# Two 64x64 products in two quarters of TensorE: a second set of operands in the other half of the partitions

## The chip, the cores and the metric

The kernel runs on one core of a Trainium2 chip. The metric is the device time of one execution in microseconds (us). The kernel before was timed three times, and once more under the profiler. The profile's engine names are PE (TensorE's matmuls), PEld (its weight loads), DVE (VectorE), ACT (ScalarE), POOL (GpSimd) and SP (SyncE, which here issues nearly all DMAs).

## The reference, cut to what matters

The reference is one inference step of a decoder layer with two branches, a gated delta rule and a sparse attention, for a prompt of 256 tokens and 8 x 8 sampled tokens. One input projection feeds both branches, and two output projections and a last one follow. Nearly all of TensorE's work is in these projections.

The change touches the delta rule alone, and in it the triangular system of each chunk and head:

```python
a_strict = jnp.where(strict, jnp.einsum('bhnid,bhnjd->bhnij', kb, k) * decay, 0.0)
rhs = jnp.concatenate([v * beta[..., None], kb * jnp.exp(G)[..., None]], axis=-1)
sol = lax.linalg.triangular_solve(a_strict, rhs, left_side=True, lower=True, unit_diagonal=True)
```

There are 32 value heads. Everything is in float32.

## The kernel before, in words

**The stream.** TensorE's main work is a stream of weight blocks of 128 columns, each in two halves (`stream`, line 379). SyncE loads a half into one of the `raw` buffers (`load_ahead`, 351), ScalarE and VectorE split it into a high and a low part, `whi` and `wlo` (`split_ahead`, 364), and 24 matmuls of 128x128 by 320 tokens add it up in a PSUM bank `pm`. A block's `done` function then reads the bank.

**Side work.** Everything else is written as Python generators. Twice per half (`side_round`, 297) each generator may emit its next step. The kernel keeps a clock of its own (`Clock`, 74) that books every instruction at an estimated cost, a DMA issue on SyncE at 0.55 us among them (172). A step that has yielded a time is taken up again when this clock's TensorE has reached it. A step that needs PSUM banks takes them from a ring of six, `ps` (`need`, 283, and `psum`, 277), and waits while the number that it asks for is not idle by the clock. `force` (321) is for the stream: where a `done` function needs a buffer that side work still holds, it runs the side steps at once, until the buffer is free. All engines work strictly in the order in which the program emits, so whatever a forced step waits for, the stream waits for too.

**The delta rule's groups.** The heads are handled in eight groups of two key heads (four value heads). In a group the stream brings two blocks of k, two of q, four of z and four of v. The prompt is cut in two chunks of 128, so a group has eight 128x128 triangular matrices of the prompt, and four more of the sampled tokens whose blocks are 16x16 and fit in the diagonal blocks of 32. `kq_gen` (1743) makes these twelve matrices in the tile `BT`, and then spawns `inverse` (1835), which leaves the transposed inverses in `XT`.

**The inverse.** It works by blocks:

- The four 32x32 diagonal blocks of the twelve matrices (48 of them) go through DRAM (`d_b`) into 48 partitions of the tile `blk`, and GpSimd inverts them by forward substitution in the tile `Xt` (`X` in the profile): 31 pairs of multiply and subtract. The inverses go out to DRAM twice, as `d_x[0]` and, transposed, as `d_x[1]`.
- Then SyncE loads what TensorE needs: `BO`, the 64x64 block off the diagonal, and `BD`, the two 32x32 blocks off the diagonal (both from `d_o`), `XT`'s diagonal blocks from `d_x[1]`, and `XB` from `d_x[0]`, the inverse of the upper 64x64 block, not transposed. `BO`, `BD`, `Q1` are slices of the tile `blk`, and `XB`, `Q2` of `Xt`. One fill by GpSimd clears a 32x32 corner of `XB`.
- Step 1 multiplies `BD` with `XB`'s diagonal blocks: 16 products of 32x32, in two quarters of the array in turn (rows 0 to 31 with columns 32 to 63, rows 64 to 95 with columns 96 to 127). Both write one bank, and ScalarE copies the result to `Q1`.
- Step 2 finishes the two 64x64 inverses: three products of 32x32 per matrix, 24 in all. Two give blocks of `XT`, the third the lower left block of `XB`. ScalarE copies them with the sign turned.
- Step 3 multiplies `BO` with `XB`: eight products of 64x64, all with rows 0 to 63 and columns 64 to 127. ScalarE copies the result to `Q2`, partitions 64 to 127.
- Step 4 multiplies `Q2` with `XT`'s lower diagonal block: eight products of 64x64, all with rows 64 to 127 and columns 0 to 63. ScalarE copies them with the sign turned to `XT`.

Which rows of the array a product takes is set by the partitions of its two operands, which columns by the PSUM partitions of its result.

**What follows.** `prompt_chain` (1968) and `sample_chain` (2045) of the group's two key heads start once `XT` is there. At their end they give back `vt` and, for the fourth use, `XT`. `v_gen` (1937) needs a free `vt` (there are two) and gives back the `vf` buffers (there are three) into which the convolution has written v. `v_done` (1693) takes a `vf` buffer for every v block and forces one where none is free. The tiles `blk` and `Xt` exist once, and so do `BT` and `XT`.

Of the kernel before, what the change touches and what calls it, by code (L numbers as in the profile page):

```python
# [11 lines left out]
AF = mybir.ActivationFunctionType  # L12
# [189 lines left out]
class Kernel:  # L202
# [1632 lines left out]
    def inverse(self, g, G):  # L1835
        nc = self.nc
        BT = G["BT"]
        d_b, d_x, d_o = self.d_b[g % 2], self.d_x[g % 2], self.d_o[g % 2]
        yield self.ready(BT)
        for k in range(4):  # L1840
            nc.sync.dma_start(d_b[k].rearrange("m j i -> j m i"), BT[32 * k:32 * k + 32, :, 32 * k:32 * k + 32])
        nc.sync.dma_start(d_o[:, :, 0:64], BT[0:64, 0:8, 64:128])
        for o in (0, 64):
            nc.sync.dma_start(d_o[o // 2:o // 2 + 32, :, 64:96], BT[o:o + 32, 0:8, o + 32:o + 64])
        self.BT.put(BT)
        yield
        yield from self.need(self.inv)
        tiles = blk, Xt = self.inv.get()
        yield self.idle(blk, Xt)
        nc.sync.dma_start(blk[0:48], d_b.rearrange("k m j i -> (k m) (j i)"))  # L1850
        nc.gpsimd.memset(Xt[0:48], 0.0)
        nc.gpsimd.memset(Xt[0:48, 0:1024:33], 1.0)
        yield
        X = Xt[0:48].rearrange("p (i c) -> p i c", c=32)
        B = blk[0:48].rearrange("p (j i) -> p j i", i=32)
        for j in range(31):
            n, m = 31 - j, j + 1
            t = self.tmp[:, 0:n * m].rearrange("p (i c) -> p i c", c=m)
            bv = B[:, j, j + 1:32].rearrange("p (i o) -> p i o", o=1).to_broadcast([48, n, m])
            xv = X[:, j:j + 1, 0:m].to_broadcast([48, n, m])  # L1860
            self.tt(t, bv, xv, OP.mult, eng=nc.gpsimd)
            self.tt(X[:, j + 1:32, 0:m], X[:, j + 1:32, 0:m], t, OP.subtract, eng=nc.gpsimd)
            if j % 4 == 4 - 1:
                yield self.clock.last - 3.6
        nc.gpsimd.tensor_copy(blk[0:48].rearrange("p (c i) -> p c i", i=32), X.rearrange("p i c -> p c i"))
        yield
        while not self.XT.free:
            yield
        XT = G["XT"] = self.XT.get()
        XB = Xt[:, 0:512].rearrange("p (m c) -> p m c", c=64)  # L1870
        Q2 = Xt[:, 512:1024].rearrange("p (m c) -> p m c", c=64)
        BO = blk[:, 0:512].rearrange("p (m c) -> p m c", c=64)
        BD = blk[:, 512:768].rearrange("p (m c) -> p m c", c=32)
        Q1 = blk[:, 768:1024].rearrange("p (m c) -> p m c", c=32)
        nc.sync.dma_start(d_x[0].rearrange("k m i c -> (k m) (i c)"), Xt[0:48])
        nc.sync.dma_start(d_x[1].rearrange("k m i c -> (k m) (i c)"), blk[0:48])
        yield max(self.clock.last, self.idle(XT))
        nc.gpsimd.memset(XB[0:32, :, 32:64], 0.0)
        nc.sync.dma_start(BO[0:64], d_o[:, :, 0:64])
        for o in (0, 64):  # L1880
            nc.sync.dma_start(BD[o:o + 32], d_o[o // 2:o // 2 + 32, :, 64:96])
        for k in range(4):
            s = slice(32 * k, 32 * k + 32)
            nc.sync.dma_start(XT[s, :, s], d_x[1][k].rearrange("m i c -> i m c"))
            if k < 3:
                o = 32 * (k % 2)
                nc.sync.dma_start(XB[s, :, o:o + 32], d_x[0][k, 0:8].rearrange("m i c -> i m c"))
        yield
        yield from self.need(self.ps_side)
        p = self.psum()  # L1890
        pv = p[:, 0:256].rearrange("p (m c) -> p m c", m=8)
        for m in range(8):
            for o in (0, 64):
                self.mm(pv[o + 32:o + 64, m, :], BD[o:o + 32, m, :], XB[o:o + 32, m, 0:32], skip=True)
        for o in (32, 96):
            self.act(Q1[o:o + 32], pv[o:o + 32])
        self.ps_side.put(p)
        yield
        yield from self.need(self.ps_side)
        p = self.psum()  # L1900
        pv = p.rearrange("p (e m c) -> p e m c", e=2, m=8)
        for m in range(8):
            for o in (0, 64):
                self.mm(pv[o:o + 32, 0, m, :], Q1[o + 32:o + 64, m, :], XT[o + 32:o + 64, m, o + 32:o + 64], skip=True)
            self.mm(pv[32:64, 1, m, :], XT[32:64, m, 32:64], Q1[32:64, m, :], skip=True)
        for o in (0, 64):
            self.act(XT[o:o + 32, 0:8, o + 32:o + 64], pv[o:o + 32, 0], AF.Copy, scale=-1.0)
        self.act(XB[32:64, :, 0:32], pv[32:64, 1], AF.Copy, scale=-1.0)
        self.ps_side.put(p)
        yield  # L1910
        yield from self.need(self.ps_side)
        p = self.psum()
        pv = p.rearrange("p (m c) -> p m c", m=8)
        for m in range(8):
            self.mm(pv[64:128, m, :], BO[0:64, m, :], XB[0:64, m, 0:64], skip=True)
        self.act(Q2[64:128], pv[64:128])
        self.ps_side.put(p)
        yield
        yield from self.need(self.ps_side)
        p = self.psum()  # L1920
        pv = p.rearrange("p (m c) -> p m c", m=8)
        for m in range(8):
            self.mm(pv[0:64, m, :], Q2[64:128, m, :], XT[64:128, m, 64:128], skip=True)
        self.act(XT[0:64, 0:8, 64:128], pv[0:64], AF.Copy, scale=-1.0)
        self.ps_side.put(p)
        self.inv.put(tiles)
        G["T"] = 4
        self.inverses += 1
# [454 lines left out]
```

## Time and profile before

| | us |
|---|---|
| median of three runs | 2191.76 |
| the three runs | 2191.92, 2191.76, 2189.55 |
| profiled execution | 2190.04 |
| its span, from the first instruction to the last | 2188.3 |
| PE busy in the span | 2157.9 |
| granted TensorE clock | 0.998 |

All instructions stand under line 61 in this profile, because one helper issues them; so they are told apart by engine, operation, and tiles: `ps<-X,blk 64*64 64x64` is a matmul that writes a `ps` bank from the tiles `X` and `blk`, over 64 rows and 64 columns of the array, with 64 columns streamed. Of the inverse, step 1 is `ps<-X,blk 32*32`, step 2 `ps<-XT,blk` and `ps<-blk,XT`, step 3 `ps<-X,blk 64*64`, and step 4 `ps<-XT,X`. A row of a timeline gives the start, the extent up to the last end, engine, operation and count; in brackets stands the idle time before it and what ended it. The ends of matmuls are modelled by the profile: they overlap, so an extent is longer than the time that an instruction keeps the next one off.

### The profile page before, as it was taken

The numbers are of one execution on the slowest core, as the hardware profiler recorded it, in microseconds if no ns is written. First come the engines' busy times: TensorE is split into PE (matmuls) and PEld (weight loads), VectorE is DVE, ScalarE is ACT, GpSimd is POOL, SyncE is SP. The second block draws the span as 40 slices with busy tenths as digits, with TensorE's granted clock in tenths as the row PEclk, the third lists the DMA queues.
The fourth block names the chain that finished last, engine by engine and source line by source line (L and its number), as shares of the span: only waits on it lengthen the run. The fifth ranks groups of instructions, "written<-read, shape, count | busy, mean of one in ns | idle before, by whom it ended". The sixth has DMA issues, their size and how long they took to land.

```text
span 2188.3 us, 43683 instructions
## 1 busy us (share of the span) xinstructions
PE 2157.9 (99%) x17151; PEld 2041.2 (93%) x17151; DVE 1384.4 (63%) x2807; ACT 1002.9 (46%) x2207; POOL 458.2 (21%) x624
## 2 busy tenths in 40 slices
PE   7999999999999999999999999999999999999997
PEld 6889988999888999899999999999999999999997
DVE  4665447789644477777777777777756545545543
ACT  3225464343343455474646464646445434233343
POOL 1000100000000008361717171717270000000000
PEclk9999999999999999999999999999999999999999
DMA  9985549765666667686768686867786966655562
GB/s 333 354 281 151 155 120 264 218 188 142 186 209 203 192 170 196 169 217 186 217 177 219 178 220 177 219 178 212 184 233 187 279 194 201 177 151 155 154 183 87
DMA packets 709839, 433.14 MB, mean 198 GB/s; under 512 B 67936, under 2 KB 697024, under 8 KB 707328
## 3 DMA queue, kind: packets, MB, share of 16 engines
q1 hardware_dynamic: 705536, 407.67, 66.1%
q0 software_dynamic: 3616, 21.02, 2.8%
q8 instruction: 135, 2.21, 0.4%
q10 hardware_dynamic: 480, 1.65, 0.2%
q14 instruction: 72, 0.59, 0.1%
HBM read 382.09 MB, written 47.89 MB: 196 GB/s over the span
## 4 chain that ended last, share of the span: by engine, by line
PE 67%; issue 23%; DVE 5%; DMA 3%; ACT 1%; SPq 0%; DVEq 0%; POOL 0%; POOLq 0%
PE pm L61 51%; PE ps L61 17%; DVE S L61 2%; DMA raw<-in_w_ada_dram 1%; DVE ps L61 1%; ACT ot L61 1%; DVE wlo L61 1%; DVE w L61 0%; DMA raw<-in_w_in_dram 0%; DMA cst<-in_conv_w_dram 0%; ACT vt L61 0%; SPq L61 0%; ACT whi L61 0%; DVE sc L61 0%; DMA c<-in_c_sample_dram 0%
## 5 line engine op out<-in xcount | busy, mean ns | idle before, releaser
L61 PE MATMUL pm<-xh,whi 128*128 128x320 f32 x3284 | 1004.4, 319 | 2.0 <-ACT whi L61 1.7
L61 PE MATMUL pm<-xl,whi 128*128 128x320 f32 x3284 | 971.6, 309 | 0.3 <-DVE xl L61 0.3
L61 DVE TENSOR_TENSOR wlo<-raw,whi 128x1024 fp32r<-128x1024 f32 x474 | 596.4, 1265 | 311.1 <-ACT whi L61 294.4
L61 PEld LDWEIGHTS pm<-xh,whi 128*128 128x128 f32 x3284 | 617.3, 188 | 34.3 <-issue 25.5
L61 PEld LDWEIGHTS pm<-xl,whi 128*128 128x128 f32 x3284 | 617.5, 188 | 1.5 <-DVE xl L61 0.8
L61 ACT ACTIVATE whi<-raw 128x1024 fp32r<-128x1024 f32 x474 | 497.9, 1058 | 158.7 <-PE pm L61 141.4
L61 PE MATMUL pm<-xh,wlo 128*128 128x320 f32 x3284 | 553.4, 309 | 0.0
L61 PEld LDWEIGHTS pm<-xh,wlo 128*128 128x128 f32 x3284 | 499.4, 188 | 0.0
L61 POOL TENSOR_TENSOR X<-X,tmpx 48x31 f32<-48x31 f32 (+15 forms) x248 | 184.0, 742 | 19.4
L61 POOL TENSOR_TENSOR tmpx<-blk,X 48x31 f32<-48x31 f32 (+15 forms) x248 | 156.4, 631 | 53.1 <-DMA blk<-d_b 21.7
L61 PE MATMUL pm<-y1h,whi 128*128 128x320 f32 x512 | 151.3, 309 | 1.1 <-ACT y1h L61 1.1
L61 PE MATMUL pm<-y1l,whi 128*128 128x320 f32 x512 | 151.2, 308 | 0.1
L61 DVE SCALAR_TENSOR_TENSOR ps<-xp,cs,ps 128x344 f32<-128x344 f32 x192 | 111.5, 581 | 6.8
L61 POOL TENSOR_TENSOR sc<-sc,mh 128x6 f32<-128x6 f32 (+1 forms) x24 | 43.6, 1815 | 328.6 <-DVE ct L61 136.6
L61 POOL TENSOR_TENSOR rfin<-rfin,mh 128x3 f32<-128x3 f32 x1 | 0.8, 848 | 486.7 <-DVE rfin L61 486.7
L61 PEld LDWEIGHTS pm<-y1h,whi 128*128 128x128 f32 x512 | 95.9, 187 | 1.3 <-ACT y1h L61 1.3
L61 PEld LDWEIGHTS pm<-y1l,whi 128*128 128x128 f32 x512 | 96.0, 187 | 0.3 <-DVE y1l L61 0.3
L61 PE MATMUL pm<-y1h,wlo 128*128 128x320 f32 x512 | 85.4, 308 | 0.0
L61 PEld LDWEIGHTS pm<-y1h,wlo 128*128 128x128 f32 x512 | 77.8, 187 | 0.0
L61 DVE SCALAR_TENSOR_TENSOR S<-S,gtr,ps 128x128 f32<-128x128 f32 x256 | 67.5, 344 | 0.1
L61 ACT ACTIVATE a<-ps 128x256 f32<-128x256 f32 (+3 forms) x96 | 50.1, 557 | 37.8 <-PE ps L61 36.6
L61 ACT ACTIVATE xp<-pm 128x256 f32<-128x256 f32 (+1 forms) x128 | 32.0, 303 | 69.7 <-PE pm L61 69.7
(360 smaller groups left out, 2317.5 us busy)
## 6 DMA issues: line engine op xcount, KB each, us to landing
raw<-in_w_in_dram SPq DMA_DIRECT2D x336, 512.0 KB
raw<-in_w_pa_dram SPq DMA_DIRECT2D x64, 512.0 KB
rawx<-in_w_ada_dram SPq DMA_DIRECT2D x18, 1024.0 KB
a<-in_w_ada_dram SPq DMA_DIRECT2D x16, 1024.0 KB
S<-in_state_gdn_dram SPq DMA_DIRECT2D x32, 512.0 KB
out_dram<-S SPq DMA_DIRECT2D x32, 512.0 KB
raw<-in_w_pb_dram SPq DMA_DIRECT2D x32, 512.0 KB
raw<-in_w_out_dram SPq DMA_DIRECT2D x32, 512.0 KB
```

What stands on the lines that cost most here:

```text
L61: made = fn(*args, **kw)
```

## The change

The eight prompt matrices are split: for matrices 4 to 7 the operands of steps 3 and 4 lie in the other half of the partitions. `Q2` shrinks to 256 columns of all 128 partitions: matrices 0 to 3 in partitions 64 to 127, matrices 4 to 7 in 0 to 63. The freed half of its old place holds `XE`: in partitions 64 to 127 the upper inverse of matrices 4 to 7 (what `XB` is for the others), and in partitions 0 to 63 a copy of the lower block of `XT` for them. `BO` of matrices 4 to 7 goes to partitions 64 to 127.

- Loads: `BO` comes in two halves instead of one piece, and four loads bring the diagonal blocks of `XE`. GpSimd clears two more 32x32 corners.
- Step 2: for matrices 4 to 7 the third product writes partitions 96 to 127 (for `XE`'s first part), and a fourth product writes a second bank (for `XE`'s second part): 28 products instead of 24. It asks for two banks. Five copies take the place of three, those to `XB` and `XE` ahead of those to `XT`.
- Step 3: the products alternate between rows 0 to 63 with columns 64 to 127 and rows 64 to 127 with columns 0 to 63, in one bank. One copy of 128 partitions by 256 takes the place of one of 64 by 512.
- Step 4: the products alternate between rows 64 to 127 and rows 0 to 63, both with columns 0 to 63, and so in two banks. Two copies take the place of one.

```diff
-        Q2 = Xt[:, 512:1024].rearrange("p (m c) -> p m c", c=64)
+        Q2 = Xt[:, 512:768].rearrange("p (m c) -> p m c", c=64)
+        XE = Xt[:, 768:1024].rearrange("p (m c) -> p m c", c=64)
...
+        nc.gpsimd.memset(XE[32:64, :, 0:32], 0.0)
+        nc.gpsimd.memset(XE[64:96, :, 32:64], 0.0)
-        nc.sync.dma_start(BO[0:64], d_o[:, :, 0:64])
+        for e in range(2):
+            nc.sync.dma_start(BO[64 * e:64 * e + 64, 0:4], d_o[:, 4 * e:4 * e + 4, 0:64])
...
+            o, t = 32 * (k % 2), 32 * ((k + 2) % 4)
+            nc.sync.dma_start(XE[t:t + 32, :, o:o + 32], d_x[k // 2][k, 4:8].rearrange("m i c -> i m c"))
...
-        yield from self.need(self.ps_side)
-        p = self.psum()
+        yield from self.need(self.ps_side, 2)
+        p, q = self.psum(), self.psum()
         pv = p.rearrange("p (e m c) -> p e m c", e=2, m=8)
+        qv = q[:, 0:128].rearrange("p (m c) -> p m c", m=4)
...
-            self.mm(pv[32:64, 1, m, :], XT[32:64, m, 32:64], Q1[32:64, m, :], skip=True)
+            o = 64 * (m // 4)
+            self.mm(pv[o + 32:o + 64, 1, m, :], XT[32:64, m, 32:64], Q1[32:64, m, :], skip=True)
+            if m > 3:
+                self.mm(qv[0:32, m - 4, :], Q1[96:128, m, :], XT[96:128, m, 96:128], skip=True)
+        self.act(XB[32:64, 0:4, 0:32], pv[32:64, 1, 0:4], AF.Copy, scale=-1.0)
+        self.act(XE[96:128, :, 0:32], pv[96:128, 1, 4:8], AF.Copy, scale=-1.0)
+        self.act(XE[0:32, :, 32:64], qv[0:32], AF.Copy, scale=-1.0)
         for o in (0, 64):
             self.act(XT[o:o + 32, 0:8, o + 32:o + 64], pv[o:o + 32, 0], AF.Copy, scale=-1.0)
-        self.act(XB[32:64, :, 0:32], pv[32:64, 1], AF.Copy, scale=-1.0)
...
-        pv = p.rearrange("p (m c) -> p m c", m=8)
-        for m in range(8):
+        pv = p[:, 0:256].rearrange("p (m c) -> p m c", m=4)
+        for m in range(4):
             self.mm(pv[64:128, m, :], BO[0:64, m, :], XB[0:64, m, 0:64], skip=True)
-        self.act(Q2[64:128], pv[64:128])
+            self.mm(pv[0:64, m, :], BO[64:128, m, :], XE[64:128, m, :], skip=True)
+        self.act(Q2, pv)
...
-        for m in range(8):
-            self.mm(pv[0:64, m, :], Q2[64:128, m, :], XT[64:128, m, 64:128], skip=True)
-        self.act(XT[0:64, 0:8, 64:128], pv[0:64], AF.Copy, scale=-1.0)
-        self.ps_side.put(p)
+        banks = [self.psum() for _ in range(2)]
+        for m in range(4):
+            self.mm(banks[0][0:64, 64 * m:64 * m + 64], Q2[64:128, m, :], XT[64:128, m, 64:128], skip=True)
+            self.mm(banks[1][0:64, 64 * m:64 * m + 64], Q2[0:64, m, :], XE[0:64, m, :], skip=True)
+        for e, p in enumerate(banks):
+            self.act(XT[0:64, 4 * e:4 * e + 4, 64:128], p[0:64, 0:256].rearrange("p (m c) -> p m c", m=4), AF.Copy, scale=-1.0)
+            self.ps_side.put(p)
```

More of the change, by code (lines that the diff above doesn't have):

```diff
@@ L1904, in inverse @@
                 self.mm(pv[o:o + 32, 0, m, :], Q1[o + 32:o + 64, m, :], XT[o + 32:o + 64, m, o + 32:o + 64], skip=True)
-            self.mm(pv[32:64, 1, m, :], XT[32:64, m, 32:64], Q1[32:64, m, :], skip=True)
+            o = 64 * (m // 4)
[5 more added lines that the diff above has]
+        self.act(XE[0:32, :, 32:64], qv[0:32], AF.Copy, scale=-1.0)
         for o in (0, 64):
             self.act(XT[o:o + 32, 0:8, o + 32:o + 64], pv[o:o + 32, 0], AF.Copy, scale=-1.0)
-        self.act(XB[32:64, :, 0:32], pv[32:64, 1], AF.Copy, scale=-1.0)
         self.ps_side.put(p)
+        self.ps_side.put(q)
         yield
@@ L1912, in inverse @@
         p = self.psum()
-        pv = p.rearrange("p (m c) -> p m c", m=8)
-        for m in range(8):
+        pv = p[:, 0:256].rearrange("p (m c) -> p m c", m=4)
+        for m in range(4):
             self.mm(pv[64:128, m, :], BO[0:64, m, :], XB[0:64, m, 0:64], skip=True)
-        self.act(Q2[64:128], pv[64:128])
+            self.mm(pv[0:64, m, :], BO[64:128, m, :], XE[64:128, m, :], skip=True)
+        self.act(Q2, pv)
         self.ps_side.put(p)
         yield
-        yield from self.need(self.ps_side)
-        p = self.psum()
-        pv = p.rearrange("p (m c) -> p m c", m=8)
-        for m in range(8):
-            self.mm(pv[0:64, m, :], Q2[64:128, m, :], XT[64:128, m, 64:128], skip=True)
-        self.act(XT[0:64, 0:8, 64:128], pv[0:64], AF.Copy, scale=-1.0)
-        self.ps_side.put(p)
+        yield from self.need(self.ps_side, 2)
+        banks = [self.psum() for _ in range(2)]
[5 more added lines that the diff above has]
+            self.ps_side.put(p)
         self.inv.put(tiles)
```

## The prediction, made before the result was known

> **What bounds the kernel now.** I read the page first: span, busy time, and the chain that ended last.
>
> ```profile
> span 2188.3 us, 43683 instructions
> PE 2157.9 (99%) x17151; PEld 2041.2 (93%) x17151; DVE 1384.4 (63%) x2807; ACT 1002.9 (46%) x2207; POOL 458.2 (21%) x624
> PE 67%; issue 23%; DVE 5%; DMA 3%; ACT 1%; SPq 0%; DVEq 0%; POOL 0%; POOLq 0%
> ```
>
> TensorE is busy for all but 30 us, and 90% of the chain is TensorE or the issue of its instructions. But that is an average over stages, so next I read the table of stages, cut at the first product of an inverse. There are eight inverses, about 109 us apart.
>
> ```profile
> 1210.20:1319.40 109.20, 108.78 (x873) 104.25 (x874) 83.39 (x198) 61.62 (x167) 51.17 (x69) 1.00 0.75 201
> ```
>
> The columns are the length, then the busy times of PE, PEld, DVE, ACT and POOL. PE idles 0.42 us in a stage of 109, at the full clock (1.00). In these stages a microsecond of PE work that goes away should come off the end, unless a new wait takes its place. So I read PE's timeline around one inverse.
>
> ```profile
> 1319.35 0.69 PE L61 MATMUL ps<-X,blk 32*32 32x32 f32 x32
> 1319.98 0.41 PE L61 MATMUL pm<-xh,whi 128*128 128x320 f32 x1
> ...
> 1324.52 1.14 PE L61 MATMUL ps<-X,blk 64*64 64x64 f32 x16
> 1325.59 0.41 PE L61 MATMUL pm<-xh,whi 128*128 128x320 f32 x1
> ```
>
> Columns: start, extent, operands, count. An f32 product shows as two instructions, so x16 is the eight products of a step, x32 the sixteen of step 1. Step 1 already alternates between two quarters (rows 0 to 31 and 64 to 95): 32 instructions hold PE from 1319.35 to 1319.98, 0.63 us. Steps 3 and 4 stay in one quarter each: the 16 instructions of step 3 hold PE for 1.07 us. The group rows show that both steps extend over the same time in all eight inverses: 9.1 us each, 1.14 per step.
>
> ```profile
> L61 PE MATMUL ps<-XT,X 64*64 64x64 f32 x128 | 9.1, 221 | 0.0
> L61 PE MATMUL ps<-X,blk 64*64 64x64 f32 x128 | 9.1, 221 | 0.0
> ```
>
> **The change part by part.** *Steps 3 and 4.* Narrow cuts of the timeline give the spacing of single instructions:
>
> ```profile
> 1324.52 0.27 PE L61 MATMUL ps<-X,blk 64*64 64x64 f32 x1
> 1324.52 0.33 PE L61 MATMUL ps<-X,blk 64*64 64x64 f32 x2
> 1319.35 0.21 PE L61 MATMUL ps<-X,blk 32*32 32x32 f32 x1
> 1319.35 0.22 PE L61 MATMUL ps<-X,blk 32*32 32x32 f32 x2
> ```
>
> In one quarter every further 64x64 instruction adds (1.14 - 0.27) / 15 = 0.058 us. In step 1 the second instruction, in another quarter, adds 0.01, and on average one adds (0.69 - 0.21) / 31 = 0.0155, so a pair takes 0.031. That is about half of 0.058, which is what one 32-column instruction should take alone: a pair costs what one costs. After the change steps 3 and 4 alternate in the same manner, 8 rounds of 0.058 in place of 16: 8 x 0.058 = 0.464 less, and 0.01 for the partner: 0.455 us per step, 0.91 per inverse, 16 x 0.455 = **7.3 us**. At worst the quarters don't overlap: 0.
>
> Step 3's two quarters differ in rows and in columns, like step 1's. Step 4's differ in rows only; both write PSUM partitions 0 to 63, in two banks. The nearest row for that is the state update of the sample chain: four strips of 32 rows, each over all 128 columns, into four banks.
>
> ```profile
> 911.55 0.59 PE L61 MATMUL ps<-w,kq 128*128 128x256 f32 x2
> 911.76 0.38 PE L61 MATMUL ps<-w,kq 128*128 128x256 f32 x1
> 912.07 1.15 PE L61 MATMUL ps<-w,ktok 32*128 32x256 f32 x16
> ```
>
> A 256-column instruction that follows another adds 0.59 - 0.38 = 0.21; sixteen in a row would take over 3.3 us, and they took 1.15. Strips that share columns do overlap, four deep, so step 4 gets its full share.
>
> A rule speaks against step 3. The Trainium skill, "TensorEngine Tiling (Array Packing)", section "Gotcha 1: PSUM Pressure", says that different row tiles cannot access the same PSUM bank at once; step 3 now writes one bank from two row tiles. By that rule step 3 would stay at 1.07 us and half of the gain would go. Step 1 of the kernel before does just that (one bank, rows 0 to 31 and 64 to 95) and its pairs overlap at 0.0155 each, so this trace does not agree for outputs in different partitions.
>
> *Step 2* gets four more 32x32 products, 8 instructions, in the second half of its rounds.
>
> ```profile
> 893.98 0.22 PE L61 MATMUL ps<-XT,blk 32*32 32x32 f32 x2
> 894.00 0.21 PE L61 MATMUL ps<-blk,XT 32*32 32x32 f32 x1
> ...
> 894.49 0.19 PE L61 MATMUL ps<-blk,XT 32*32 32x32 f32 x1
> 894.61 0.42 PE L61 MATMUL pm<-xh,whi 128*128 128x320 f32 x1
> ```
>
> 48 instructions in rounds of three hold PE for 0.63 us, as long as step 1's 32 in rounds of two. The third in a round is free; I take the fourth as free too. If each took a place alone: 8 x 0.031 = 0.25 per inverse, 2.0 in all.
>
> *Copies out of PSUM (ScalarE).* Step 2 goes from three copies to five (the three to XB and XE half as long), step 3 from one of 64x512 to one of 128x256, step 4 from one to two of half the length.
>
> ```profile
> 1322.68 0.76 ACT L61 ACTIVATE XT<-ps 32x256 f32<-32x256 f32 x2 [0.49 <-PE ps L61]
> 1323.47 0.37 ACT L61 ACTIVATE X<-ps 32x256 f32<-32x256 f32 x1
> 1325.69 0.59 ACT L61 ACTIVATE X<-ps 64x512 f32<-64x512 f32 x1 [1.85 <-PE ps L61]
> 1328.72 0.59 ACT L61 ACTIVATE XT<-ps 64x512 f32<-64x512 f32 x1 [1.35 <-PE ps L61]
> ```
>
> Step 2: 2 more of at most 0.37, step 3: 0.2 less, step 4: 2 x 0.37 - 0.59 = 0.15 more: about 0.6 us of ScalarE per inverse at most, 5 us in all. It lies in waits of ScalarE for PE (1.85 and 1.35 us before these very copies), while PE has weight matmuls to go on with. With no cover it would be those 5 us.
>
> *GpSimd* gets two more fills of 32x128, at most 0.30 each; it is busy 51 of 109 us in a stage.
>
> *SyncE's queue* gets five more issues per inverse: four loads of XE, and BO in two halves.
>
> ```profile
> 1307.75 2.64 SPq L61 DMA_DIRECT2D blk<-d_o  x3
> 1310.48 0.54 SPq L61 DMA_DIRECT2D XT<-d_x  x1
> 1311.07 0.47 SPq L61 DMA_DIRECT2D X<-d_x  x1
> ...
> 1314.18 0.47 SPq L61 DMA_DIRECT2D X<-d_x  x1
> 1314.70 0.46 SPq L61 DMA_DIRECT2D XT<-d_x  x1
> ```
>
> The seven loads of XT and XB take from 1310.48 to 1315.16, 0.67 each; five more are about 3.3 us. Behind them in the queue stand a store to d_z, the next weight loads (raw) and the stores of the next group's BT. I take this as hidden on the queue's side: SyncE mostly waits for DVE to give raw buffers back.
>
> ```profile
> SPq L61 <- DVE wlo L61: 888.2, 302, 12.3
> ```
>
> With that cover gone, 8 x 3.3 = 26 us would show. On the chain's side nothing hides it: XT of a group comes up to 3.3 us later, so the chains and then the freeing of vt and vf come later. What is late next is `v_done`, which forces a free vf buffer for the fourth v block of the next group.
>
> ```profile
> 1361.74 0.82 PE L61 MATMUL ps<-ident,vf 128*128 128x128 f32 x6
> 1369.73 0.49 ACT L61 ACTIVATE xp<-pm 128x256 f32<-128x256 f32 x2
> ```
>
> The transposes that free vf start at 1361.74, and the fourth block is read out at 1369.73: about 8 us of room against a delay of 3. I take 0 here. When the force does bite, its price is in the trace: it did in the first group.
>
> ```profile
> 926.34 0.44 PE L61 MATMUL ps<-ident,vf 128*128 128x128 f32 x2 [0.53 <-DVE S L61]
> 927.38 0.66 PE L61 MATMUL ps<-ident,vf 128*128 128x128 f32 x4 [0.60 <-DVE S L61]
> ```
>
> That is 1.13 us of idle PE, 9.0 us if every group paid it.
>
> *Moved places.* Steps move by a side round or so, and a burst that meets another burst of side work saves one opening, or costs one where it parts from it: the first instruction of step 3 extends over 0.27, each further one adds 0.058. I allow this 0.2 us per inverse either way, 1.6 in all, and take 0.3 of loss into the sum.
>
> The sum: 7.3 - 0.3 = **7.0 us less**. The profiled execution took 2190.04 us (span 2188.3 and 1.7 around it), so 2183.0. The median of the runs is 2191.76, 1.7 above; the four executions shown average 2190.8, and 7.0 below that is 2183.8. I predict **2184**. A change under 0.2% (4.4 us) counts as none.
>
> **The rivals.** *Half the gain* (0.11): one of the two products doesn't overlap, or step 2 pays its 2.0 and some of the delays show. Then 7.3 / 2 - 0.3 = 3.4 less: about 2187.5, no measurable change. For it: neither 64x64 pairing stands in the trace as such. Against: the pairs of step 1 and the strips above. The bank rule of the skill would end here; I give it 0.03 of this.
>
> *The gain is paid back by a forced wait* (0.12). The later XT makes the chains late, `v_done` forces, and PE waits 1.13 us in up to every group: 9.0 - 7.0 = 2.0 slower at the full price, 2.5 faster if half of the groups pay: 2188 to 2193, with 2190.5 in the middle. For it: the first group shows the force. Against: the 8 us of room.
>
> *Slower* (0.09): PE itself waits for the loads. Step 1 stands in PE's queue at 1319.35, and everything behind it waits, the weight stream too. The last load of XB that it reads is issued at 1314.18 now; one more BO half and two XE loads ahead of it (3 x 0.67 = 2.0) make that 1316.2. How long a load takes to land is bounded by the first inverse:
>
> ```profile
> L61 SPq DMA_DIRECT2D blk<-d_b x8: 445/916/1317, 820.0 to 1566.5; - x8
> L61 POOL TENSOR_TENSOR tmpx<-blk,X x248: 230/554/1687, 824.7 to 1626.9; 48x31 f32<-48x31 f32 x8, 48x87 f32<-48x87 f32 x8, 48x135 f32<-48x135 f32 x8, 48x175 f32<-48x175 f32 x8
> ```
>
> Issued at 820.0, used at 824.7: at most 4.7 us. Then step 1 could start only at 1316.2 + 4.7 = 1320.9, 1.55 us late: 8 x 1.55 = 12.4 us lost against 7.0 gained, 5.4 slower, about 2196. It decides from the point where the landing takes over 1319.35 - 1316.2 = 3.2 us while step 1 keeps its place. Against it: step 1 is emitted only after the kernel's own clock has the loads landed, and that clock charges each issue 0.55 us, so the step should move back with them.
>
> *The change doesn't do what it says* (0.03): the quarters don't overlap at all: 0 to 2.0 slower, 2191 to 2193.
>
> **How the numbers follow.** The forecast has 0.60. 0.05 is left for a better fit of the moved bursts (over 9 us less). Faster by over 0.2%: 0.60 x 0.95 + 0.05 + 0.02 of the half case, 0.64. Same: the remaining 0.03, the half case's 0.09, the payback's 0.10 and 0.03 of no overlap: 0.25. Slower: 0.09 and 0.02 of the payback: 0.11. The forecast's own range is 2181 to 2187 (the executions before spread over 2.4 us; 1.6 for the places). The range of 8 in 10 runs from 2180 (every term at its best: 2189.55 - 7.3 - 1.6) to 2191, which takes in the half case and most of the payback.
>
> **What would show it.** Steps 3 and 4 with extents of 0.68 (0.27 + 7 x 0.058 + 0.01) in place of 1.14; their two groups together 10.9 us in place of 18.2; step 2 still 0.63 to the next pm row; stages of 108.3 in place of 109.2, with 0.4 us of idle PE as before. Wrong: an idle entry of PE before step 1 that names a DMA, idle PE before the vf transposes in later groups, 1.14 left on one of the steps, or stages of 109 with the products shorter.

## The result and the profile after

The changed kernel takes **2179.37 us** (median of six runs, 2178.61 to 2179.90) against 2191.52 (median of six runs of the kernel before, 2189.55 to 2191.92): a ratio of 0.9947, 95% interval 0.9934 to 0.9959, or 12.15 us less. The profiled execution took 2179.01 against 2190.04, 11.0 less. In a later repetition (experiment 7) one execution of the changed kernel was slow, 2767 us at a mean granted clock of 0.71, and is left out of the figures there. The forecast was 7.0 less; the time lies 1.6 us below the forecast's own range (2181 to 2187) and 0.6 below the low end of the range of 8 in 10. So the questions are whether the products gave what the sum said, and where 4 to 5 us more came from.

The page of the changed kernel, its span, busy times and the chain that ended last:

```profile
span 2177.3 us, 43942 instructions
PE 2149.5 (99%) x17215; PEld 2035.2 (93%) x17215; DVE 1385.0 (64%) x2807; ACT 1005.1 (46%) x2231; POOL 458.3 (21%) x640
PE 72%; issue 23%; DMA 2%; DVE 2%; SPq 1%; ACT 0%; DVEq 0%; POOL 0%; POOLq 0%; ACTq 0%
```

PE is busy for 8.4 us less and the span is 11.0 shorter, so some of the gain is not PE work that went away. In the chain, DVE's share fell from 5% to 2%.

PE's timeline around steps 3 and 4 of one inverse of the changed kernel (start, extent, operands, count):

```profile
1213.23 0.68 PE L61 MATMUL ps<-X,blk 64*64 64x64 f32 x16
1213.84 0.41 PE L61 MATMUL pm<-xh,whi 128*128 128x320 f32 x1
...
1215.79 0.27 PE L61 MATMUL ps<-XT,X 64*64 64x64 f32 x1
1215.80 0.27 PE L61 MATMUL ps<-X 64*64 64x64 f32 x1
...
1216.40 0.42 PE L61 MATMUL pm<-xh,whi 128*128 128x320 f32 x1
```

Step 3 holds PE from 1213.23 to 1213.84, 0.61 us, where it held it for 1.07 before: 0.46 less. In step 4 the two products of a pair start 0.01 apart, and the next weight matmul starts 0.61 after the step's start, as behind step 3, though step 3 writes one bank and step 4 two. The group rows say the same of all eight inverses; step 4 now has two names, since half of its products take both operands from `X`:

```profile
L61 PE MATMUL ps<-X,blk 64*64 64x64 f32 x128 | 5.4, 224 | 0.0
L61 PE MATMUL ps<-XT,X 64*64 64x64 f32 x64 | 5.4, 224 | 0.0
L61 PE MATMUL ps<-X 64*64 64x64 f32 x64 | 5.4, 224 | 0.0
```

That is 0.68 per step, and 10.8 us for the two steps together (the two names of step 4 run side by side), where it was 18.2. The stage, cut from one step 1 to the next as before:

```profile
1206.28:1313.61 107.33, 107.33 (x879) 103.26 (x878) 83.62 (x198) 62.11 (x170) 51.31 (x71) 1.00 0.76 203
```

It is 107.33 us long. Cut in the same way, from step 1 to step 1, the stage of before is 109.16 (the prediction's window of 109.20 is 0.04 wider). The products explain 2 x 0.46 = 0.92 of the 1.83 by which it is shorter; the other 0.9 is not in any product. Only the three middle stages of the seven between the eight inverses are alike in this way; the others differ in what else falls into them. The view that shows where the 0.9 may have been is the list of waits of PEld, the weight loads of PE (total, times, longest); first the kernel before, then the changed one:

```profile
PEld pm L61 <- ACT whi L61: 3.3, 6, 0.6
PEld ps L61 <- DVE w L61: 2.3, 6, 0.4
...
PEld ps L61 <- ACT whi L61: 1.0, 5, 0.2
```

```profile
PEld pm L61 <- ACT whi L61: 1.7, 2, 1.1
...
PEld ps L61 <- DVE w L61: 0.4, 1, 0.4
```

The weight loads waited 6.6 us in these three rows before and 2.1 after. The row of the stage before had shown 0.42 us of idle PE, less than the 1.1 us of weight waits that the trace has in the same stage (0.19, 0.39 and 0.55): the modelled end of a matmul can lie past the moment at which the next one could have started, and then it covers a part of a wait.

The waits before were five or six of each sort, about one per stage. Nothing in the edit touches how `whi` and `w` are made, so the order of the work is what may have moved them; the experiments test it.

### The profile page after: what moved, and what is told of

Read it like the earlier page. It is cut to its first block, busy times and chain, and to the rows that moved or that the text cites. A ratio compares the mean times of both kernels' runs of the same rounds, so it can differ in the third digit from the quotient of the medians.

```text
span 2177.3 us, 43942 instructions
## 1 busy us (share of the span) xinstructions
PE 2149.5 (99%) x17215; PEld 2035.2 (93%) x17215; DVE 1385.0 (64%) x2807; ACT 1005.1 (46%) x2231; POOL 458.3 (21%) x640
## 4 chain that ended last, share of the span: by engine, by line
PE 72%; issue 23%; DMA 2%; DVE 2%; SPq 1%; ACT 0%; DVEq 0%; POOL 0%; POOLq 0%; ACTq 0%
PE pm L61 55%; PE ps L61 17%; DMA raw<-in_w_ada_dram 1%; SPq L61 1%; DVE S L61 1%; DVE wlo L61 0%; DMA c<-in_c_sample_dram 0%; DMA out_dram<-S 0%; ACT ot L61 0%; ACT whi L61 0%; DMA cst<-in_conv_w_dram 0%; DMA zf<-d_z 0%; DVE sga L61 0%; DVE w L61 0%; DVEq L2394 0%
## 5 line engine op out<-in xcount | busy, mean ns | idle before, releaser
L61 DVE TENSOR_TENSOR wlo<-raw,whi 128x1024 fp32r<-128x1024 f32 x474 | 589.3, 1251 | 295.2 <-ACT whi L61 272.5
L61 POOL TENSOR_TENSOR X<-X,tmpx 48x31 f32<-48x31 f32 (+15 forms) x248 | 174.5, 704 | 19.4
L61 POOL TENSOR_TENSOR tmpx<-blk,X 48x31 f32<-48x31 f32 (+15 forms) x248 | 161.9, 653 | 51.6 <-DMA blk<-d_b 33.4
```

The costliest lines, as they stand in the source:

```text
L61: made = fn(*args, **kw)
```

## The experiments

**The theories.** *M*: the products give about 7.1 (16 x 0.46 less a little in step 2), and 4 to 5 come from places: step 2 ends later on the kernel's own clock (five copies), step 3 misses its side round, and it and much of what follows stands a round later. *P*: all of the 11 to 12 us comes from the alternation of the quarters. *L*: it comes from the later loads. *R*, formed after the first four runs: a moved step takes waits away in one place and makes them in another, so nothing is won in sum. W and C, two more rivals, stand in the expectation of experiment 7. Every time is set against the kernel before, timed on the same chip. A difference to the changed kernel is taken to its first median, 2179.37; its repetition in experiment 7 lies 1.2 higher, so such differences are uncertain by that much. How many steps stand elsewhere was counted in the kernels' programs, not in a trace: the delta rule's side work has 360 steps that compute, and a step has moved when it is emitted in another round of the weight stream.

**1. The same products, not in turns.** In steps 3 and 4 the four products of the first quarter are emitted, then the four of the second.

```diff
         for m in range(4):
             self.mm(pv[64:128, m, :], BO[0:64, m, :], XB[0:64, m, 0:64], skip=True)
+        for m in range(4):
             self.mm(pv[0:64, m, :], BO[64:128, m, :], XE[64:128, m, :], skip=True)
```

(and in the same way in step 4.)

> The changed kernel with the products of steps 3 and 4 in the order of the quarters (four in the first, then four in the second), all else and the places of the steps as in the changed kernel. Theory M (the spacing of the products gives 7.1 us, and the other 4 to 5 us of the 12 come from step 3 and what follows it standing a side round later in the stream, which takes away waits of PE's weight queue for DVE w and ACT whi): steps 3 and 4 take 1.31 us again from the instruction before them to the one after, 16 x 0.46 = 7.4 us are lost, about 2186.8, and the waits stay away (PEld for DVE w near 0.4 us, for ACT whi near 1.7). Rival P (all of the gain comes from the alternation, directly or because the results are there earlier): near the kernel before, 2190 to 2192, with the waits back.

It took 2184.02 (2182.78 to 2184.94) against 2190.83, ratio 0.9968 [0.9956, 0.998]: 4.6 slower than the changed kernel, 2.8 faster than M had it, and well below the 2190 of P, whose waits did not come back either. The products were expected to queue up behind each other as in one quarter. PE's timeline of one step 4 shows that they don't:

```profile
1219.42 0.50 PE L61 MATMUL ps<-XT,X 64*64 64x64 f32 x5
1219.71 0.27 PE L61 MATMUL ps<-X 64*64 64x64 f32 x1
1219.76 0.22 PE L61 MATMUL ps<-XT,X 64*64 64x64 f32 x1
1219.82 0.22 PE L61 MATMUL ps<-X 64*64 64x64 f32 x1
1219.82 0.22 PE L61 MATMUL ps<-XT,X 64*64 64x64 f32 x1
1219.88 0.22 PE L61 MATMUL ps<-X 64*64 64x64 f32 x1
1219.88 0.22 PE L61 MATMUL ps<-XT,X 64*64 64x64 f32 x1
1219.93 0.45 PE L61 MATMUL ps<-X 64*64 64x64 f32 x5
1220.32 0.41 PE L61 MATMUL pm<-xh,whi 128*128 128x320 f32 x1
```

`XT,X` is the first quarter, eight instructions of program order ahead of the eight of the second. The records show the first of the second quarter start after five of the first. So the step holds PE from 1219.42 to 1220.32, 0.90 us: 0.29 more than in turns (16 x 0.29 = 4.6, as much as the difference), and 0.17 less than in one quarter. Its weight loads wait 1.9 us for `whi`, and its order of the side work is that of the changed kernel.

The trace of this kernel also has the one wait that the "slower" rival was made of, in the first inverse:

```profile
893.00 0.69 PE L61 MATMUL ps<-X,blk 32*32 32x32 f32 x30 [0.88 <-DMA X<-d_x]
```

A load of `XB` came 0.88 us late there. The changed kernel has no such wait in its two traces; experiment 4 has one of 0.62 us, ahead of step 1 at 1536.50. The mechanism exists, with little room.

**2. The changed kernel at the old places.** After step 2 the next step is due 0.5 us of the kernel's clock earlier.

```diff
-        yield
+        yield self.clock.last - 0.5
```

> The changed kernel, but the generator yields half a microsecond less after step 2, so that step 3 is taken up in the same side round as in the kernel before, and with it step 4 and the chains. Theory M: the products keep their 0.85 us, the waits come back (PEld for DVE w 2 us, ACT whi 3 to 4 us in all), stages of 108.3 us, about 2183.5. Rival P: as the changed kernel, 2179 to 2180, stages of 107.3.

2182.89 (2182.05 to 2186.07), ratio 0.9965 [0.9952, 0.9979]: 3.5 slower than the changed kernel (2.4 against its repetition), as M said. Steps 3 and 4 keep their 0.68, and the waits come back:

```profile
PEld pm L61 <- ACT whi L61: 3.9, 6, 1.2
...
PEld ps L61 <- DVE w L61: 2.0, 5, 0.4
```

P falls here: with the alternation untouched, a fifth to a third of the gain has gone, and the like stage (shown below) is 108.26 long, where P had 107.3.

The third row of the waits, of `ps` for `whi`, has not come back with the places, so it hangs on the products too. It cost PE nothing: step 4 starts 0.24 us behind the matmul ahead of it in experiment 4, with that wait, and just so with the old products in experiment 7, in stages without it.

**3. The kernel before, with step 3 later.** The same line of the kernel before, the other way.

```diff
-        yield
+        yield self.clock.last + 0.5
```

> The kernel before, but the generator yields half a microsecond more after step 2, so that step 3 is taken up one side round later, as in the changed kernel; no product, load or copy is changed. Theory M: steps 3 and 4 keep 1.31 us, waits of PEld for DVE w and ACT whi fall from 6.6 to about 2 us, stages of 108.2 in place of 109.2, about 2187.3. Rival P: no change, 2190.5 to 2192.5. Rival L (the later loads and the longer queue of SyncE do it): no change either.

2194.05 (2189.89 to 2197.15), ratio 1.0015 [1.0006, 1.0024]: slower than before, where M had 2187.3 and P no change. The wait for `w` did go (2.3 to 0.4), but a new one stands in PE's timeline, ahead of a transpose of the convolution's state, and with it a stretch in which the granted clock (the third figure from the end) is half:

```profile
1181.25 0.54 PE L61 MATMUL ps<-ident,cst 92*128 92x92 f32 x2 [3.22 <-DMA cst<-in_state_conv_dram]
```

```profile
1180.77:1184.19 3.42, 2.94 (x12) 2.97 (x13) 3.42 (x10) 1.33 (x4) 3.19 (x4) 0.50 1.16 321
```

In that stretch weight matmuls start 0.27 us apart instead of 0.15; by an estimate from these two spacings, about 1.3 us are lost. The wait and the stretch together, 4.5 us, are more than the 2.7 by which this profiled execution is longer between the first step 1 and the last matmul (1287.75 against 1285.06). Ten of its eleven executions have a mean granted clock of 0.996 or 0.997, against 4 of 22 of the kernel before (the others 0.998); the eleventh took 2189.89. So the sign of this result may rest on one wait for a DMA and the clock behind it.

"A round later" alone is then not enough to tell. This kernel's order was laid beside the others': over half of the 360 steps of the delta rule's side work stand elsewhere than in the kernel before, and over half elsewhere than in the changed kernel. It was no test of the changed kernel's places.

**4. The loads alone.** The kernel before with the change's DMAs and fills: `BO` in two halves (to the old place), four loads of `XE`, two fills. The extra data is read by nothing.

```diff
-        nc.sync.dma_start(BO[0:64], d_o[:, :, 0:64])
+        nc.gpsimd.memset(XE[32:64, :, 0:32], 0.0)
+        nc.gpsimd.memset(XE[64:96, :, 32:64], 0.0)
+        for e in range(2):
+            nc.sync.dma_start(BO[0:64, 4 * e:4 * e + 4], d_o[:, 4 * e:4 * e + 4, 0:64])
...
+            o, t = 32 * (k % 2), 32 * ((k + 2) % 4)
+            nc.sync.dma_start(XE[t:t + 32, :, o:o + 32], d_x[k // 2][k, 4:8].rearrange("m i c -> i m c"))
```

> The kernel before with the change's extra issues alone: BO in two halves (both to the old place), the four loads of XE (step 3's copy later overwrites half of it, nothing reads it) and the two fills; products and copies as before. Theory M: SyncE's extra 3 us per inverse are hidden and step 3 keeps its place, so no change, 2190.5 to 2192.5, waits as before. Rival L (the extra issues move the chains, and that gives the 4 us): about 2187.5.

2190.20 (2188.63 to 2191.55), ratio 0.9995 [0.9986, 1.0004]: no difference. L falls, and five issues of SyncE per inverse are hidden, as the prediction had them, but for the 0.62 us named above. Its order differs from that of the kernel before in about a tenth of the steps, and is the order of experiment 2, step for step.

**5. All of the change but the second quarter.** Loads, fills, step 2's four extra products, its five copies and two banks, step 4's two copies; steps 3 and 4 with all eight products in the old quarter. The order is that of the changed kernel.

```diff
-            self.mm(pv[0:64, m, :], BO[64:128, m, :], XE[64:128, m, :], skip=True)
-        self.act(Q2, pv)
+        self.act(Q2[64:128], pv[64:128])
...
-        yield
+        yield self.clock.last - 0.2
...
-            self.mm(banks[1][0:64, 64 * m:64 * m + 64], Q2[0:64, m, :], XE[0:64, m, :], skip=True)
```

(the loops run over eight matrices instead of four; the -0.2 keeps step 4 in its round.)

> All of the change but the second quarter: the loads, fills, the four products more in step 2, the five and the two copies and the two banks as in the changed kernel, so that every step stands where it stands there; but all products of steps 3 and 4 read the old operands in the old quarter (the second set is loaded and written and not read). Theory M (places): steps 3 and 4 take 1.31 us again, 16 x 0.46 = 7.4 us more than the changed kernel, about 2186.8, some 4 below the kernel before although not one product overlaps; PEld's waits for DVE w near 0.4 us and for ACT whi below 2. Rival P (only the alternation helps, and the places of the steps are an effect of the shorter products on the chip): 2190 to 2192, waits as before. Rival R (the run with step 3 moved in the kernel before is typical: a moved step takes waits away in one place and makes them in another, so nothing is won in sum): 2190 to 2194 with the DVE w waits gone and others in their place.

2188.51 (2186.43 to 2190.98, 11 runs) against 2190.24, ratio 0.9989 [0.998, 0.9998]: 1.7 less. M had 2186.8, P and R 2190 and more; none is hit. The waits are those of the changed kernel (0.4 for `w`, 1.8 for `whi`), where P had them as before. Its stages are shorter by all that M asks:

```profile
1211.80:1320.06 108.26, 108.26 (x880) 104.18 (x879) 83.73 (x198) 62.16 (x170) 51.32 (x71) 1.00 0.75 199
```

The missing 2 us show in its trace long before the first inverse, which begins at 894.22 instead of 891.55. About 0.9 of them are there when the weights of the first stage have been waited for (this kernel with its granted clock right behind, then the changed one):

```profile
53.83 0.42 PE L61 MATMUL pm<-raw,cT 128*32 128x256 f32 x4 [1.84 <-DMA raw<-in_w_ada_dram]
```

```profile
55.12:58.54 3.42, 3.42 (x15) 3.42 (x15) 0.90 (x3) 0.00 (x0) 0.00 (x0) 0.50 1.08 370
```

```profile
52.97 0.85 PE L61 MATMUL pm<-raw,cT 128*32 128x256 f32 x12 [1.58 <-DMA raw<-in_w_ada_dram]
```

The largest part is the clock: it is half for 3.4 us, and the twelve matmuls of the first weight blocks take 3.13 us from 54.83 on where the changed kernel's take 1.87, 1.3 lost. The remaining 0.5 is a wait for a DMA at 772.94. From the first step 1 to the last matmul the kernel takes 1281.13, 3.9 less than the kernel before, which is M's 4. Of its eleven executions eight have a mean clock under 0.998, against 3 of 15 of the kernel before; the three others took 2187.23 to 2188.51. Whether the others lost time at the same spot isn't known. At this point the worth of the places was open between 1.7 and 4.

**6. Still later.** The changed kernel with the step after step 2 due 2 us later.

```diff
-        yield
+        yield self.clock.last + 2.0
```

> The changed kernel with step 3 taken up 2 us later still, which in the kernel's own order brings the substitution of the next group to another place in the stage as well. It measures how far places alone move the time. Theory M gives no sign for it: the products keep 0.85 us, so 2183.5 (the time with the places of before) plus or minus 4; waits of PEld say which. Rival P: 2179 to 2180, as the changed kernel.

2182.40 (2181.12 to 2183.71), ratio 0.9962 [0.9949, 0.9976]: 3.0 slower than the changed kernel, with the products as fast. The wait for `w` is gone, but the one that the prediction feared, ahead of the transposes that free `vf`, has spread to other groups:

```profile
L61 PE MATMUL ps<-ident,vf 128*128 128x128 f32 x96 | 13.9, 275 | 2.5 <-DVE S L61 2.5
```

This kernel pays 2.5 us there where the kernel before and the changed one pay 1.1. The half of R by which places win and lose holds; the other half, that nothing is won in sum, is met neither here nor in experiment 5 (2188.51, where R had 2190 to 2194). P, which had 2179 to 2180 here, misses again.

**7. The changed kernel's places with the old products, and the changed kernel again.** Experiment 4 with one line more:

```diff
-        yield
+        yield self.clock.last + 0.2
```

All 360 steps then stand where they stand in the changed kernel (and in experiments 1 and 5), while products and copies are those of before.

> The kernel before with the change's loads and fills, whose extra data nothing reads (this alone took 2190.2), and one more edit: the step after step 2 is due 0.2 us of the kernel's own clock later. With it all 360 steps of the delta rule's side work stand at the same weight half, in the same order, as in the changed kernel; products and copies are those of before (at +0.5 without the loads, in the kernel that took 2194.05, 207 of the 360 stood elsewhere). Theory M (the places alone are worth what the three other corners show between the first step 1 and the last matmul, 3.9 us): 1281.2 between these two rows instead of 1285.1, about 2186.3, stages of 108.2. Rival W (the places are worth only the 1.7 that the medians of the kernel with all products in one quarter show): 2188.5. Rival C (it is the extra copies and products that open the gaps, not the places): 2190.2, stages of 109.15.

> The changed kernel itself beside the kernel before on the same chip: 2179.4, ratio 0.995, if the first comparison holds; the difference to the run with the same places and the old products should be 16 x 0.46 = 7.4 by theory M, 9.1 by rival W.

The old products at the changed kernel's places took **2185.31** (2183.84 to 2187.28) against 2190.22, ratio 0.9978 [0.9968, 0.9988]: 4.9 less, without one product changed. M's 2186.3 lies within its runs, W's 2188.5 and C's 2190.2 lie above all nine. The changed kernel took 2180.53 (median of five, 2179.26 to 2182.13) against the same 2190.22, ratio 0.9956 [0.9943, 0.9969].

The stages, each with the first row cut at its own step 1: experiment 4, experiment 2, and then the old products at the new places:

```profile
1208.58:1317.72 109.14, 108.73 (x872) 104.20 (x871) 82.96 (x198) 61.64 (x167) 51.71 (x71) 1.00 0.75 201
```

```profile
1207.36:1315.62 108.26, 107.83 (x879) 103.30 (x878) 83.38 (x198) 61.69 (x170) 51.60 (x71) 1.00 0.76 202
```

```profile
1208.17:1316.40 108.23, 108.23 (x872) 104.15 (x871) 83.72 (x198) 61.96 (x167) 51.33 (x71) 1.00 0.74 199
```

| stage, us | products in one quarter | products in two |
|---|---|---|
| old places | 109.14 | 108.26 |
| the changed kernel's places | 108.23 | 107.33 |

Down each column the order alone changes, along each row the products and what serves them: 0.91 and 0.93 for the places, 0.88 and 0.90 for the products. In these like stages the two add up, and each is half of the gain. At the new places PE's idle time in a stage is zero in these rows (108.23 busy of 108.23).

Where the 0.91 lies can be read in the same stage, from start to start of PE's rows, ahead of `w` and ahead of `whi` in experiment 4, and ahead of `whi` at the new places:

```profile
1238.89 0.90 PE L61 MATMUL pm<-xh,wlo 128*128 128x320 f32 x5
1239.91 0.70 PE L61 MATMUL ps<-w,ktok 128*128 128x256 f32 x2
...
1258.37 0.46 PE L61 MATMUL pm<-xh,wlo 128*128 128x320 f32 x2
1259.11 0.41 PE L61 MATMUL pm<-xh,whi 128*128 128x320 f32 x1 [0.29 <-ACT whi L61]
```

```profile
1256.83 1.19 PE L61 MATMUL pm<-xh,wlo 128*128 128x320 f32 x7
1257.85 0.31 PE L61 MATMUL pm<-xh,whi 128*128 128x320 f32 x1
```

Seven weight matmuls take 1.02 us where nothing waits, 0.146 each. In experiment 4 five take 1.02 ahead of `w`, 0.29 too long, and two take 0.74 ahead of `whi`, 0.45 too long. That is 0.74 of the 0.91. The like stages at the new places have neither wait.

Over the whole inverse part the first step 1 and the last matmul bound the time; first the kernel before, then the old products at the new places, then the changed kernel:

```profile
891.40 0.69 PE L61 MATMUL ps<-X,blk 32*32 32x32 f32 x32
...
2176.46 0.27 PE L61 MATMUL ps<-ident,sgb 128*128 128x128 f32 x1
```

```profile
891.87 0.69 PE L61 MATMUL ps<-X,blk 32*32 32x32 f32 x32
...
2172.11 0.27 PE L61 MATMUL ps<-ident,sgb 128*128 128x128 f32 x1
```

```profile
891.55 0.69 PE L61 MATMUL ps<-X,blk 32*32 32x32 f32 x32
...
2165.39 0.27 PE L61 MATMUL ps<-ident,sgb 128*128 128x128 f32 x1
```

1285.06, 1280.24 and 1273.84 us: the places give 4.8, and what remains of the change 6.4. Experiment 2 takes 1277.68, so in the other order of the two steps it is 7.4 for the products and 3.8 for the places: over the whole they add up only to within 1.0. The 6.4 is less than the 7.4 of the products (16 x 0.46), because part is given back. Step 2 takes 0.03 more in each inverse (it holds PE for 0.66 instead of 0.63), 0.2 in all; and a new wait stands in the changed kernel's timeline of PE, which is not in the one with the old products and copies (the changed kernel, the old products at the new places, and then experiment 5):

```profile
982.57 0.42 PE L61 MATMUL pm<-xh,whi 128*128 128x320 f32 x1 [0.85 <-ACT whi L61]
```

```profile
982.78 0.31 PE L61 MATMUL pm<-xh,whi 128*128 128x320 f32 x1
```

```profile
986.31 0.41 PE L61 MATMUL pm<-xh,whi 128*128 128x320 f32 x1 [0.98 <-ACT whi L61]
```

PE comes to this block earlier than ScalarE has it ready, and waits 0.85. So 7.4 - 0.2 - 0.85 = 6.35, against 6.4 measured. The faster products are not what makes this wait: experiment 5 has it too, with all products in one quarter and PE no earlier at this block (91.1 us after its first step 1, against 90.9 at the same places with the old copies). ScalarE's split of the block starts 91.0 us after the first step 1 there, 89.9 in the changed kernel, and 89.5 with the old copies. So the wait comes with the change's other parts, the extra products and copies of step 2 and the two copies of step 4, which experiment 5 shares with the changed kernel; which of them makes ScalarE later isn't settled. That the difference between the two kernels isn't the 7.4 expected of the last run fits this: it is 4.8 in the medians of this chip (5.9 with the first comparison's 2179.37) and 6.4 in the traces. The medians of one kernel on two occasions differ by 1.2, so they can't tell these apart. No order that was tried beats the changed kernel; the two kernels at the same products but other places (2182.9 and 2182.4) are slower.

## Why the prediction was right and wrong

**What bounds the kernel: half right.** A microsecond of PE work that went away did come off the end. But the sentence that PE idles 0.42 us in a stage took PE's busy time at its word. The list of the weight loads' waits had 6.6 us in three rows of the kernel before, and the prediction didn't read it. There was more to be had than products, and it was visible.

**Steps 3 and 4: right.** 0.455 per step forecast, 0.46 measured (1.07 to 0.61), extents of 0.68 as forecast, the two steps together 10.8 against 10.9. The chosen price of a pair (one instruction's 0.058) holds for both pairings. The bank rule of the Trainium skill, "TensorEngine Tiling (Array Packing)", "Gotcha 1: PSUM Pressure", would have left step 3 at 1.07; it is at 0.61 with two row tiles in one bank, in different partitions, so this trace doesn't agree.

**Step 2: right within its bounds.** Free by the forecast, 0.03 per inverse measured, of at most 0.25.

**Copies, fills and issues: right but for one wait.** Loads and fills by themselves gave 2190.20 against 2190.83. The copies' own time doesn't show in the like stages: at the same places and with the products in one quarter a stage is 108.23 with three copies in step 2 and 108.26 with five. (The three differences of ScalarE's sum add up to 0.7, not 0.6; nothing hangs on it.) Once, ahead of the block shown above, ScalarE was late and PE waited 0.85. What the copies did beyond that was to move step 3, and that belongs to the next term.

**Moved places: wrong, in size and in sign.** This is the step that failed: "I allow this 0.2 us per inverse either way, 1.6 in all, and take 0.3 of loss into the sum." The places alone gave 4.9 in the medians and 4.8 in the traces, 0.91 in each like stage. The term was sized by the opening of a burst (0.27 against 0.058), as if a step that moves took only its own opening along. In fact the order of the chains changed: a quarter to a third of the 360 steps stand elsewhere, by whether one counts by weight half or by round. And what that order sets is above all waits: whether PE meets `w` and `whi` before VectorE and ScalarE have them ready. These are 0.74 of the 0.91 in a like stage; the remaining 0.17 is about the size that the prediction allowed for openings. The weight loads' waits with the old products at the new places:

```profile
PEld pm L61 <- ACT whi L61: 0.6, 1, 0.6
...
PEld ps L61 <- DVE w L61: 0.4, 1, 0.4
...
PEld ps L61 <- ACT whi L61: 0.4, 2, 0.2
```

They are 1.4 us instead of 6.6. That the difference of 5.2 is near the gain of 4.8 is partly luck: of the 1.1 us of such waits in a like stage 0.74 show between PE's starts. With 4.8 of gain in that term, the forecast's own sum would have been 7.3 + 4.8 = 12.1 less, against 11.0 in the profiled execution; the rest is step 2 (0.2) and the wait for ScalarE above (0.85).

**The rivals.** *Half the gain*: no. *Forced wait*: not in the changed kernel, whose row for the `vf` transposes is as before; but at other places it came (experiment 6), so the caution was in place. The changed kernel's row:

```profile
L61 PE MATMUL ps<-ident,vf 128*128 128x128 f32 x96 | 13.4, 274 | 1.1 <-DVE S L61 1.1
```

*Slower, by waiting loads*: not in the changed kernel; 0.88 us once in experiment 1 and 0.62 once in experiment 4. *No overlap*: no.

**The range.** It ended 0.6 us too high, because its best case took 1.6 for the places. Kernels with the same products lie 3.5 us apart (2179.4, 2182.4, 2182.9), those with the old products 8.7 (2185.3, 2190.2, 2190.8 and 2194.05, leaving experiment 5 aside; the last holds the half clock of experiment 3). A term of 4 to 5 us either way is what these runs support.

**What stays open.** Which of the moved steps removes which wait was not taken apart, nor which of the change's copies and products makes ScalarE late at the one block. Experiment 5, at the same places, gained only 1.7 in the medians: its stages are as short as M asks, and its profiled execution lost 2.7 before the first inverse, 1.3 of it at half clock, but only that one execution was seen.

## What to carry to other kernels

Independent f32 products of 64x64 whose operands can be put in different halves of the partitions cost one per pair here; emit them in turns. The one or two more copies out of PSUM were hidden in the like stages, where TensorE has other work. When the order is planned by estimated costs, any edit that changes an estimate is two edits: price the second by reading the weight loads' waits and not only PE's idle time (here 6.6 us of them stood against 4.8 won), and measure it with a kernel that has the new order and the old work. The comparison is worth making only if the orders are compared step by step first: a delay that looked the same (experiment 3) had over half of its steps elsewhere and was no such test. And read the granted clock of each profile before a difference of 1 or 2 us is put down to the edit.

## What the runs showed of the hardware that was not expected

PE starts matmuls of another quarter ahead of earlier ones of a busy quarter: in experiment 1 the first of the second quarter started after five of the eight that stand ahead of it in the program, and the step took 0.90 us, between the 0.61 of products in turns and the 1.07 of one quarter. The text ahead of the prediction says that all engines work strictly in the order in which the program emits; for PE's starts within such a step that is not so. The Trainium skill, "TensorE: Matmul & The Clock Gate", "Part 3: Packing small matmuls — row/col tiling", states that matmuls keep program order in start and end; these records don't agree in their starts (the ends are modelled by the profile, and nothing here tests them).

Two row quarters that write one bank in different partitions (step 3) take as long as two that write two banks (step 4): 0.61 us each for 16 instructions.

In three of the profiles (experiments 3, 4 and 5) the granted clock was half for 3.41 us in the middle of the work, each time beside an idle time of PE: 3.22, 1.80 and 1.84 us. Weight matmuls then started 0.27 us apart instead of 0.15. An idle time of 1.86 us in experiment 6, at the same spot as that of experiment 5, had no such stretch behind it, so these runs give no rule for when it comes.
